# Edge-to-node feature sums by one-hot products: longer alternation of blocks and products, other PSUM banks, GpSimd work in short pieces

## The chip, the cores and the metric

The kernel runs on one core of a Trainium2 chip. The metric is the device time of one execution in microseconds. Of the kernel before, seven runs were timed: the median is 342.38 us, the lowest 340.65 and the highest 344.02.

## What is computed

```python
# num_nodes, num_edges, dim = 4096, 65536, 128; float32 features
output = np.zeros((num_nodes, dim), dtype=np.float32)
for i in range(len(edge_index_src)):
    output[edge_index_dst[i]] += node_features[edge_index_src[i]]
```

Each edge adds the feature row of its source node to the row of its destination node. Both are random numbers below 4096, that is, one of 32 blocks of 128 nodes.

## The kernel before

The kernel has no gather. It sorts the edges so that TensorE can do the sum as a matrix product. **Pass 1** (up to about 70 us) moves each edge to a row that belongs to its destination block, and **pass 2** moves it on by source block. What then remains of an edge is a pair of numbers below 128, source and destination within their blocks. VectorE turns such numbers into one-hot matrices: a comparison of a row 0..127 with each number (`onehot`, L201).

The **main loop** goes over 32 slots (from L585), one for each of the 32 destination blocks. For a slot TensorE does two things.

- `blocks(k)`, k from 0 to 7, is four matmuls 128x128 of one-hots (bf16, L532). They fill one PSUM bank `psa` with four count matrices (how many edges go from source to destination, for four source blocks). ScalarE copies the bank to SBUF as fp32r, `a[:, k, :]` (L534).
- `product(k)` is two matmuls 128x512 in fp32r (L539): the node features (`xr`, in a high and a low part) times `a`. They add up in the bank `pso` over four slots' worth of source blocks: 64 matmuls, then ScalarE copies the bank out (`evacuate`, L298). Later `finish` transposes it with four matmuls into `psx` (L305), ScalarE copies that to `rows` (L307), and SyncE sends it to HBM.

The products lag by one slot: in slot s TensorE works on the blocks of slot s and the products of slot s-1. The order is written by hand: blocks k and k+1 (eight matmuls), products k and k+1 (four matmuls), four times over. `finish` stands behind the first such pair of steps. So TensorE changes between blocks and products four times each way in a slot.

VectorE makes the two one-hot tensors of slot s+1 while slot s runs (`onehots`, two instructions 128x4096, L201). They go to two tiles in turn, so VectorE has to wait until the blocks of slot s-1 have been read.

**Pass 2 runs inside the main loop.** Its 32 positions are cut into `GROUPS` of 4, 4, 4, 4, 8 and 8. `STEPS` says by hand in which slot a group's next step is issued. A step has a VectorE half, which is issued ahead of the slot's blocks, and a TensorE half, which is issued behind the slot's products. For a group of 4 the steps are: one-hots (`buckets4`, L473) and `payloads` (L415), with column sums (L482); scans (L489) with counting matmuls `counts_ranks` (L496, L499; ScalarE copies with L502) and `ranks` (L432); then pairs of `permutations` (VectorE, L201, to `p2a` and `p2c`) and `permuted` (TensorE, L452), followed two slots later by `quad_keys` (VectorE, L465). For a group of 8, `buckets` (32 instructions, L400) and `before_all` (L408) come first, then `running` (eleven VectorE additions, L423) with `masked` (L427) and `payloads`, then `ranks`, then four pairs. Group 0 and the first two steps of group 1 run ahead of the loop.

GpSimd has `masked` and, from group 1 on, `payloads`. One `payloads` instruction multiplies 128x3072 bf16 elements, one `masked` instruction 128x6144. They are one instruction each, or two `payloads` for a group of 8.

PSUM has eight banks, which the pool `ps` gives out by tag, with two buffers unless told otherwise: `psA` (blocks, and the counting banks `psc` of both passes) two, `pso` (products, and `pst` and `psr` of pass 1) two, `misc` (`psm`, `psb`, `psr2`, `pst2`, `psx`, `psf`) two, `psi` one, `ps2` one. A matmul that writes a bank anew waits until its last reader is done.

Of the kernel before, what the change touches and what calls it, by code (L numbers as in the profile page):

```python
# [8 lines left out]
P = 128  # L9
F32 = mybir.dt.float32  # L10
# [7 lines left out]
NB = 32  # L18
# [60 lines left out]
def _fast(ctx, tc, X, src32, dst32, out, ident, fmax, flag_i, T):  # L79
# [129 lines left out]
    def oh1s(q):  # L209

        if q % 2 == 0:
            oh1[q // 2] = sb1.tile([P, 2, NL, NB], BF16, name="oh1", tag=f"o{q // 2}")
        onehot(oh1q(q), kd[:, q], NL, NB)
        pst = ps.tile([P, 512], F32, name="pst", tag="pso")
        for j in range(NJ):
            PE.matmul(out=pst[:, j:j + 1],  # L216
                      lhsT=oh1q(q)[:, 4 * j:4 * j + 4, :].rearrange("p l b -> p (l b)"),
                      rhs=ones[:, :1], start=True, stop=True)
        sums[q] = pst
# [8 lines left out]
    def counts(q):  # L228

        cum = sb1.tile([P, NB, NL], BF16, name="cum", tag=f"c{q % 2}")  # L230
        for j0 in range(0, NJ, 4):
            n = min(4, NJ - j0)
            psc = ps.tile([P, 512], F32, name="psc", tag="psA")
            PE.matmul(out=psc[:, :n * P], lhsT=early[:],  # L234
                      rhs=oh1q(q)[:, 4 * j0:4 * (j0 + n), :].rearrange("p t b -> p (t b)"),
                      start=True, stop=j0 + n == 1)
            for j in range(max(j0, 1), j0 + n):
                PE.matmul(out=psc[:, (j - j0) * P:(j - j0 + 1) * P],  # L238
                          lhsT=sums[q][:, j - 1:j].to_broadcast([P, P]), rhs=identb[:],
                          start=False, stop=j == j0 + n - 1)  # L240
            S.activation(out=cum[:, :, 4 * j0:4 * (j0 + n)], func=RELU, bias=minus[:],  # L241
                         in_=psc[:, :n * P].rearrange("p (t b) -> p b t", b=NB))
            yield
        psr = ps.tile([P, 512], F32, name="psr", tag="pso")
        for b in range(NB):
            PE.matmul(out=psr[:, :NL], lhsT=identb[:], rhs=cum[:, b, :],  # L246
                      start=b == 0, stop=b == NB - 1)
        rank1[q] = sb2.tile([P, 4, NJ, 2], BF16, name="rank1", bufs=3)
        for k in range(2):
            S.copy(out=rank1[q][:, :, :, k], in_=psr[:, :NL].rearrange("p (j l) -> p l j", l=4))  # L250
# [23 lines left out]
    sbk = sb1.tile([P, NCH, NB], BF16, name="sbk")  # L274

    def move1(q, meanwhile):
        psm = ps.tile([P, 512], F32, name="psm", tag="misc")
        for l in range(4):
            t = p1[l // 2]
            n = len([j for j in range(NJ) if j * NCH + q * 4 + l < T])  # L280
            for j0, j1, m0, m1 in WIN:
                j1 = min(j1, n)
                onehot(t[:, l % 2, j0:j1, m0:m1], rank1[q][:, l, j0:j1], j1 - j0, m1 - m0, m0=m0)
            meanwhile(l)
            for j in range(n):
# [14 lines left out]

    def finish():
        for k, res in done:
            psx = ps.tile([P, 512], F32, name="psx", tag="misc")
            for i in range(4):
                PE.transpose(psx[:, i * P:(i + 1) * P], res[:, i * P:(i + 1) * P], ident[:])  # L305
            rows = sb2.tile([P, 4, P], F32, name="rows", bufs=1)
            S.copy(out=rows[:].rearrange("p i f -> p (i f)"), in_=psx[:])  # L307
            nc.sync.dma_start(
                out=out[4 * k * P:4 * (k + 1) * P, :].rearrange("(i p) f -> p i f", p=P),
                in_=rows[:])  # L310
        done.clear()
# [56 lines left out]
    first = [sum(GROUPS[:g]) for g in range(len(GROUPS))]  # L368
    keys2 = {}

    def pass2(g):


# [7 lines left out]
        def flat2(t):  # L381
            return t.rearrange("p c i s k -> p c (i s k)")
# [19 lines left out]
                    in_=sbk[:, :, ds].rearrange("p c (i k) -> p c i k", k=kk))  # L402

        def before_all():
            psb = ps.tile([P, 512], F32, name="psb", tag="misc")
            for h in range(2):
                for c in range(NH):
                    PE.matmul(out=psb[:, h * W:(h + 1) * W], lhsT=before[:],  # L408
                              rhs=flat2(T2["o"])[:, h * NH + c], start=c == 0, stop=c == NH - 1)
            for h in range(2):  # L410
                S.copy(out=flat2(T2["c"])[:, h * NH], in_=psb[:, h * W:(h + 1) * W])

        def payloads():
            for i in range(gk):
                (V if g == 0 else G).tensor_tensor(out=T2["v"][:, :, i], in0=T2["o"][:, :, i], op=OP.mult,  # L415
                                in1=sa[:, :, None, d0 + kk * i:d0 + kk * i + kk].to_broadcast(
                                    [P, NCH, NB, kk]))

        def running():
            cums = flat2(T2["c"]).rearrange("p (h c) w -> p h c w", h=2)  # L420
# [3 lines left out]
                                op=OP.add)  # L424

        def masked():
            G.tensor_tensor(out=flat2(T2["c"]), in0=flat2(T2["c"]), in1=flat2(T2["o"]), op=OP.mult)  # L427

        def ranks():
            psr = ps.tile([P, 512], F32, name="psr2", tag="misc")  # L430
            for s in range(NB):
                PE.matmul(out=psr[:, :NCH * gd], lhsT=identb[:],  # L432
                          rhs=T2["c"][:, :, :, s, :].rearrange("p c i k -> p (c i) k"),
                          start=s == 0, stop=s == NB - 1)
            T2["r"] = sb2.tile([P, gd, NCH, 2], BF16, name="rank2")
            for k in range(2):
                S.copy(out=T2["r"][:, :, :, k],  # L437
                       in_=psr[:, :NCH * gd].rearrange("p (c d) -> p d c", d=gd))
# [5 lines left out]
                    onehot(p2b[d % 4][:, cs, h * 64:h * 64 + 64], T2["r"][:, d, cs], NH, 64)  # L444

        def permuted(i):
            if i % 4 == 0:
                T2["ps2"] = ps.tile([P, 512], F32, name="ps2", tag="ps2", bufs=1)
            ps2 = T2["ps2"]
            for d in range(i, i + 2):  # L450
                for c in range(NCH):
                    PE.matmul(out=ps2[:, d % 4 * NB:(d % 4 + 1) * NB],  # L452
                              lhsT=p2b[d % 4][:, c, :], rhs=T2["v"][:, c, d // kk, :, d % kk],
                              start=c == 0, stop=c == NCH - 1)
            if i % 4 == 2:
                T2["pa"] = sb2.tile([P, NB, 4], BF16, name="pa")
                S.copy(out=T2["pa"][:],
                       in_=ps2[:, :4 * NB].rearrange("p (d s) -> p s d", d=4))
# [18 lines left out]
                in1=sbk[:, :, None, d0:d0 + 4].to_broadcast([P, NCH, NB, 4]))  # L477

        def column_sums():
            T2["p"] = ps.tile([P, 512], F32, name="pst2", tag="misc")  # L480
            for c in range(NCH):
                PE.matmul(out=T2["p"][:, c:c + 1], lhsT=flat2(T2["o"])[:, c], rhs=ones[:, :1],  # L482
                          start=True, stop=True)
# [7 lines left out]

        def counts_ranks():
            for c0 in range(0, NCH, 4):
                psc = ps.tile([P, 512], F32, name="psc2", tag="psA")
# [32 lines left out]
        return oh  # L527

    def blocks(k, oh, a):
        psa = ps.tile([P, 512], F32, name="psa", tag="psA")  # L530
        for i in range(4):
            PE.matmul(out=psa[:, i * P:(i + 1) * P], lhsT=oh[:, 0, 4 * k + i, :],  # L532
                      rhs=oh[:, 1, 4 * k + i, :], start=True, stop=True)
        S.copy(out=a[:, k, :], in_=psa[:])  # L534
# [7 lines left out]
    def flag():  # L542
# [10 lines left out]
        psf = ps.tile([P, 512], F32, name="psf", tag="misc")  # L553
# [6 lines left out]
    def run(fs):  # L560
        for f in fs:
            f()
# [22 lines left out]
    for slot in range(slots):  # L585
# [5 lines left out]
        if slot + 1 < slots:  # L591
            oh = onehots(slot + 1)
        run(st[0] for st in steps)
        a = sb1.tile([P, 8, 4 * P], F32R, name="a", tag=f"A{slot % 2}")
        if slot % 4 == 0:
            pso = ps.tile([P, 512], F32, name="pso", tag="pso")
        for k in range(0, 8, 2):
            blocks(k, cur, a)
            blocks(k + 1, cur, a)
            if prev is not None:  # L600
                product(k, *prev)
                product(k + 1, *prev)
            if k == 0:
                finish()
        if prev is not None and prev[0] % 4 == 3:
            evacuate(prev[0] // 4, prev[2])
        run(st[1] for st in steps if len(st) > 1)
# [98 lines left out]
```

## Time and profile before

| what | value |
| --- | --- |
| the profiled execution's own time | 342.22 us |
| its span, first to last instruction | 340.5 us |
| median of the seven runs | 342.38 us |
| mean granted TensorE clock | 0.969 |
| TensorE matmuls busy | 302.6 us |
| VectorE busy | 280.4 us |
| ScalarE busy | 201.6 us |
| GpSimd busy | 84.0 us |
| `product` matmuls (L539) | 512, 149.3 us busy |
| `blocks` matmuls (L532) | 1024, 81.2 us busy |
| copies of a block bank (L534) | 256, mean 591 ns |
| one-hots of a slot (L201) | 2 of 128x4096, mean 2287 and 2280 ns |

In the profile, PE is TensorE's matmuls, PEld its weight loads, DVE is VectorE, ACT ScalarE, POOL GpSimd. "L539" is a line of the kernel before. In a list of groups or a timeline, a line gives start and duration in us (or the sum of busy time and the mean), engine, line, operation, the tiles (written <- read), the shape, and the number of instructions. In square brackets stands the time for which the engine was idle before, and whose work ended that. Matmuls overlap: the duration of one is longer than the distance to the next. So distances between starts are what counts on TensorE.

### The profile page before, as it was taken

To read this page: it belongs to the slowest core of one execution; us is meant where nothing else is said; L and a number is where in the kernel's file an instruction comes from. 1 tells how busy PE (TensorE), PEld (TensorE's weight loads), DVE (VectorE), ACT (ScalarE), POOL (GpSimd) and SP (SyncE) were. 2 spreads that over 40 slices of the span, in tenths; PEclk is the share of its full clock that TensorE was granted. 3 is DMA by queue.
4 is the path that set the end of the run, shared out by engine and by line. 5 is a ranking of instruction groups with operands and counts; after the bars stand their busy time and mean duration, and the time that the engine had idled before them with its cause. 6 is when DMAs were issued, how large, how long until landed. Compare 5 with 4: busy or idle time off the path is not lost.

```text
span 340.5 us, 8629 instructions
## 1 busy us (share of the span) xinstructions
PE 302.6 (89%) x3783; PEld 239.9 (70%) x3784; DVE 280.4 (82%) x365; ACT 201.6 (59%) x389; POOL 84.0 (25%) x47
## 2 busy tenths in 40 slices
PE   0579898558879999999999999999999999999993
PEld 0368787456668678677788787778878778877772
DVE  4999999981899839868999898999999779858710
ACT  2776545014455766755755766575576676677761
POOL 6627000206006060000799000059900000000000
PEclk9999979975799999999999999999999999999999
DMA  8500000000000000100010000001000100100101
GB/s 241 128 2 5 2 3 2 2 2 0 3 2 2 2 2 2 31 2 3 0 33 2 0 6 30 0 3 33 2 1 2 33 0 2 33 2 0 33 2 33
DMA packets 8711, 5.81 MB, mean 17 GB/s; under 512 B 224, under 2 KB 8416, under 8 KB 8672
## 3 DMA queue, kind: packets, MB, share of 16 engines
q1 hardware_dynamic: 8528, 4.72, 4.8%
q8 instruction: 30, 0.49, 0.6%
q10 hardware_dynamic: 144, 0.52, 0.5%
q14 instruction: 9, 0.07, 0.1%
HBM read 3.15 MB, written 2.10 MB: 15 GB/s over the span
## 4 chain that ended last, share of the span: by engine, by line
PE 69%; DVE 19%; ACT 5%; issue 5%; DMA 1%; DVEq 0%; ACTq 0%
PE pso L539 33%; PE psa L532 15%; DVE oh L201 8%; PE ps L452 7%; PE psr L432 3%; PE psm L286 3%; DVE p L201 2%; DVE v L262 2%; ACT cum L502 2%; DMA raw<-in_edge_index_dst_dram 1%; DVE cum L423 1%; ACT cum L241 1%; PE psc L496 1%; PE psr L246 1%; PE psc L499 1%
## 5 line engine op out<-in xcount | busy, mean ns | idle before, releaser
L534 ACT CAST a<-psa 128x512 fp32r<-128x512 f32 x256 | 137.7, 591 | 46.0 <-PE psa L532 45.0
L539 PE MATMUL pso<-a,xr 128*128 128x512 f32 x512 | 149.3, 414 | 0.0
L201 DVE TENSOR_TENSOR oh<-psi,slo 128x4096 bf16<-128x4096 uint16 x32 | 73.2, 2287 | 27.9 <-PE psa L532 27.8
L539 PEld LDWEIGHTS pso<-a,xr 128*128 128x128 f32 x512 | 87.0, 189 | 11.3
L532 PE MATMUL psa<-oh 128*128 128x128 bf16 x1024 | 81.2, 220 | 1.4 <-ACT a L534 0.9
L532 PEld LDWEIGHTS <-oh 128*128 128x128 bf16 x1024 | 59.3, 98 | 29.9 <-issue 28.4
L201 DVE TENSOR_TENSOR oh<-psi,dlo 128x4096 bf16<-128x4096 uint16 x32 | 73.0, 2280 | 0.0
L415 POOL TENSOR_TENSOR v<-oh,sa 128x3072 bf16<-128x3072 bf16 x7 | 37.6, 5391 | 41.8 <-DVE oh L473 33.6
L427 POOL TENSOR_TENSOR cum<-cum,oh 128x6144 bf16<-128x6144 bf16 x2 | 23.9, 11930 | 75.7 <-ACT a L534 75.7
L201 DVE TENSOR_TENSOR p<-psi,rank 128x448 bf16<-128x448 uint16 (+3 forms) x72 | 29.2, 471 | 0.0
L241 ACT ACTIVATE cum<-psc,minus 128x512 bf16<-128x512 f32 (+1 forms) x36 | 21.8, 650 | 10.4 <-PE psc L238 9.9
L286 PE MATMUL psm<-v,p 128*128 128x64 bf16 x512 | 22.7, 202 | 5.6 <-DVE p L201 5.0
L286 PEld LDWEIGHTS <-p 128*128 128x128 bf16 x512 | 19.6, 103 | 7.5 <-DVE p L201 7.2
L201 DVE TENSOR_TENSOR p2a<-psi,rank 128x768 bf16<-128x768 uint16 x32 | 15.5, 548 | 7.2 <-ACT rank L437 7.2
L201 DVE TENSOR_TENSOR p2c<-psi,rank 128x768 bf16<-128x768 uint16 x32 | 15.5, 547 | 0.0
L238 PEld LDWEIGHTS <-sums 128*128 128x128 bf16 x126 | 10.9, 105 | 6.5 <-issue 3.2
L234 PE MATMUL psc<-oh,early 128*128 128x512 bf16 (+1 forms) x36 | 14.4, 399 | 1.0 <-ACT cum L241 1.0
L432 PEld LDWEIGHTS <-identb 128*128 128x128 bf16 x192 | 12.3, 103 | 4.2 <-issue 4.2
L190 POOL TENSOR_TENSOR xr<-xf,xr 128x512 fp32r<-128x512 f32 x8 | 11.7, 1488 | 13.4 <-ACT xr L186 13.4
L216 PE MATMUL pst<-ones,oh 128*128 128x1 bf16 x132 | 4.3, 164 | 12.0 <-DVE oh L201 12.0
L452 PEld LDWEIGHTS <-p2a 128*128 128x128 bf16 x384 | 12.8, 100 | 2.9 <-DVE p2a L201 1.8
L452 PEld LDWEIGHTS <-p2c 128*128 128x128 bf16 x384 | 12.9, 102 | 1.9 <-issue 1.6
(82 smaller groups left out, 278.0 us busy)
## 6 DMA issues: line engine op xcount, KB each, us to landing
xf<-in_node_features_dram SPq DMA_DIRECT2D x4, 512.0 KB, 7.4
out_dram<-rows SPq DMA_DIRECT2D x8, 256.0 KB, 2.3
raw<-in_edge_index_src_dram ACTq DMA_DIRECT2D x1, 512.0 KB, 4.8
raw<-in_edge_index_dst_dram SPq DMA_DIRECT2D x1, 512.0 KB, 5.1
```

What stands on the lines that cost most here:

```text
L190: G.tensor_tensor(out=xr[i // 2][:, bs, 1, :], op=OP.subtract, in0=xf[i][:, h * BX // 2:(h + 1) * BX // 2], in1=xr[i // 2][:, bs, 0, :])
L201: V.tensor_tensor(out=dst.rearrange("p i (m k) -> p i m k", k=2), in0=io.rearrange("p i (m k) -> p i m k", k=2), in1=keys2[:, :, None, :]. ...
L234: PE.matmul(out=psc[:, :n * P], lhsT=early[:], rhs=oh1q(q)[:, 4 * j0:4 * (j0 + n), :].rearrange("p t b -> p (t b)"), start=True, stop=j0 + ...
L241: S.activation(out=cum[:, :, 4 * j0:4 * (j0 + n)], func=RELU, bias=minus[:], in_=psc[:, :n * P].rearrange("p (t b) -> p b t", b=NB))
L286: PE.matmul(out=psm[:, l * 64:(l + 1) * 64], lhsT=t[:, l % 2, j, :], rhs=v1[q][:, 4 * j + l].rearrange("p k b -> p (k b)"), start=j == 0, ...
L415: (V if g == 0 else G).tensor_tensor(out=T2["v"][:, :, i], in0=T2["o"][:, :, i], op=OP.mult, in1=sa[:, :, None, d0 + kk * i:d0 + kk * i + ...
L427: G.tensor_tensor(out=flat2(T2["c"]), in0=flat2(T2["c"]), in1=flat2(T2["o"]), op=OP.mult)
L432: PE.matmul(out=psr[:, :NCH * gd], lhsT=identb[:], rhs=T2["c"][:, :, :, s, :].rearrange("p c i k -> p (c i) k"), start=s == 0, stop=s == N ...
L452: PE.matmul(out=ps2[:, d % 4 * NB:(d % 4 + 1) * NB], lhsT=p2b[d % 4][:, c, :], rhs=T2["v"][:, c, d // kk, :, d % kk], start=c == 0, stop=c ...
L532: PE.matmul(out=psa[:, i * P:(i + 1) * P], lhsT=oh[:, 0, 4 * k + i, :], rhs=oh[:, 1, 4 * k + i, :], start=True, stop=True)
L534: S.copy(out=a[:, k, :], in_=psa[:])
L539: PE.matmul(out=pso[:], lhsT=xr[s // 16][:, s % 16, v, :], rhs=a[:, k, :], start=s == 0 and v == 0, stop=s == NB - 1 and v == 1)
```

## The change

The diff has three parts.

1. **Order in the slot.** Four `blocks` (sixteen matmuls), then four `products` (eight matmuls), twice over. `finish` moves from behind the first two products to between the second four blocks and the second four products. The matmuls and their number stay.
2. **Banks.** `psA` gets four banks, `pso` and `misc` one each. In pass 1, `pst` goes to `ps2` and `pso` in turn, and `psr` to `psA`.
3. **GpSimd in pieces.** `payloads` is cut into pieces of four chunks (six of 128x512 for each 128x3072), `masked` into pieces of two chunks (twelve of 128x512). They go to a list `small`; the program issues up to seven of them in each slot, behind the VectorE halves, and what `ranks` or `permuted` needs, ahead of those. Group 0's payload stays one VectorE instruction.

```diff
@@ oh1s, counts, move1, finish, before_all, ranks, column_sums, flag: banks
-        pst = ps.tile([P, 512], F32, name="pst", tag="pso")
+        pst = ps.tile([P, 512], F32, name="pst", tag=("ps2", "pso")[q % 2], bufs=1)
-            psc = ps.tile([P, 512], F32, name="psc", tag="psA")
+            psc = ps.tile([P, 512], F32, name="psc", tag="psA", bufs=4)
-        psr = ps.tile([P, 512], F32, name="psr", tag="pso")
+        psr = ps.tile([P, 512], F32, name="psr", tag="psA", bufs=4)
-        psm = ps.tile([P, 512], F32, name="psm", tag="misc")
+        psm = ps.tile([P, 512], F32, name="psm", tag="misc", bufs=1)
...
+    small = []
+
+    def little(n=0, until=None):
+        while small and (n > 0 or any(k == until for k, _ in small)):
+            small.pop(0)[1]()
+            n -= 1
...
+        def payload(e, i, cs):
+            ds = slice(d0 + kk * i, d0 + kk * i + kk)
+            e.tensor_tensor(out=T2["v"][:, cs, i], in0=T2["o"][:, cs, i], op=OP.mult,
+                            in1=sa[:, cs, None, ds].to_broadcast([P, cs.stop - cs.start, NB, kk]))
+
         def payloads():
+            if g == 0:
+                payload(V, 0, slice(0, NCH))
+                return
             for i in range(gk):
-                (V if g == 0 else G).tensor_tensor(out=T2["v"][:, :, i], in0=T2["o"][:, :, i], op=OP.mult,
-                                in1=sa[:, :, None, d0 + kk * i:d0 + kk * i + kk].to_broadcast(
-                                    [P, NCH, NB, kk]))
+                for c in range(0, NCH, 4):
+                    small.append(((g, 1), lambda i=i, c=c: payload(G, i, slice(c, c + 4))))
...
         def masked():
-            G.tensor_tensor(out=flat2(T2["c"]), in0=flat2(T2["c"]), in1=flat2(T2["o"]), op=OP.mult)
+            for c in range(0, NCH, 2):
+                small.append(((g, 0), lambda c=c: G.tensor_tensor(
+                    out=flat2(T2["c"])[:, c:c + 2], in0=flat2(T2["c"])[:, c:c + 2],
+                    in1=flat2(T2["o"])[:, c:c + 2], op=OP.mult)))
         def ranks():
+            little(until=(g, 0))
...
         def permuted(i):
+            little(until=(g, 1))
...
     def blocks(k, oh, a):
-        psa = ps.tile([P, 512], F32, name="psa", tag="psA")
+        psa = ps.tile([P, 512], F32, name="psa", tag="psA", bufs=4)
...
         run(st[0] for st in steps)
+        little(7)
         a = sb1.tile([P, 8, 4 * P], F32R, name="a", tag=f"A{slot % 2}")
         if slot % 4 == 0:
-            pso = ps.tile([P, 512], F32, name="pso", tag="pso")
-        for k in range(0, 8, 2):
-            blocks(k, cur, a)
-            blocks(k + 1, cur, a)
+            pso = ps.tile([P, 512], F32, name="pso", tag="pso", bufs=1)
+        for k0 in (0, 4):
+            for k in range(k0, k0 + 4):
+                blocks(k, cur, a)
+            if k0 == 4:
+                finish()
             if prev is not None:
-                product(k, *prev)
-                product(k + 1, *prev)
-            if k == 0:
-                finish()
+                for k in range(k0, k0 + 4):
+                    product(k, *prev)
```

More of the change, by code (lines that the diff above doesn't have):

```diff
@@ L302, in finish @@
         for k, res in done:
-            psx = ps.tile([P, 512], F32, name="psx", tag="misc")
+            psx = ps.tile([P, 512], F32, name="psx", tag="misc", bufs=1)
             for i in range(4):
@@ L404, in before_all @@
         def before_all():
-            psb = ps.tile([P, 512], F32, name="psb", tag="misc")
+            psb = ps.tile([P, 512], F32, name="psb", tag="misc", bufs=1)
             for h in range(2):
@@ L426, in masked @@
         def masked():
-            G.tensor_tensor(out=flat2(T2["c"]), in0=flat2(T2["c"]), in1=flat2(T2["o"]), op=OP.mult)
+            for c in range(0, NCH, 2):
+                small.append(((g, 0), lambda c=c: G.tensor_tensor(
+                    out=flat2(T2["c"])[:, c:c + 2], in0=flat2(T2["c"])[:, c:c + 2],
+                    in1=flat2(T2["o"])[:, c:c + 2], op=OP.mult)))
         def ranks():
-            psr = ps.tile([P, 512], F32, name="psr2", tag="misc")
+            little(until=(g, 0))
+            psr = ps.tile([P, 512], F32, name="psr2", tag="misc", bufs=1)
             for s in range(NB):
@@ L479, in column_sums @@
         def column_sums():
-            T2["p"] = ps.tile([P, 512], F32, name="pst2", tag="misc")
+            T2["p"] = ps.tile([P, 512], F32, name="pst2", tag="misc", bufs=1)
             for c in range(NCH):
@@ L493, in counts_ranks @@
             for c0 in range(0, NCH, 4):
-                psc = ps.tile([P, 512], F32, name="psc2", tag="psA")
+                psc = ps.tile([P, 512], F32, name="psc2", tag="psA", bufs=4)
                 cs = [c for c in range(c0, c0 + 4) if c % NH]
@@ L552, in flag @@
         V.tensor_reduce(out=fall[:], in_=fmax[:, :ng + 1], op=OP.add, axis=AX.X)
-        psf = ps.tile([P, 512], F32, name="psf", tag="misc")
+        psf = ps.tile([P, 512], F32, name="psf", tag="misc", bufs=1)
         PE.matmul(out=psf[:1, :1], lhsT=fall[:], rhs=one[:], start=True, stop=True)
```

## The prediction

> **What bounds the kernel now.** I read the page first: shares, slices, chain.
>
> ```profile
> PE 302.6 (89%) x3783; PEld 239.9 (70%) x3784; DVE 280.4 (82%) x365; ACT 201.6 (59%) x389; POOL 84.0 (25%) x47
> ...
> PE   0579898558879999999999999999999999999993
> ...
> DVE  4999999981899839868999898999999779858710
> ...
> PE 69%; DVE 19%; ACT 5%; issue 5%; DMA 1%; DVEq 0%; ACTq 0%
> ```
>
> PE is full from about 120 us on, the chain of waits is mostly PE. But two engines are nearly full, so I asked for busy time in stretches of 10 us (PE, PEld, DVE, ACT, POOL, clock):
>
> ```profile
> 60.00:70.00 10.00, 6.57 (x126) 5.47 (x126) 10.00 (x21) 0.43 (x2) 2.78 (x4) 0.85 0.01 2
> ...
> 270.00:280.00 10.00, 10.00 (x85) 7.59 (x84) 6.54 (x7) 7.46 (x15) 0.00 (x0) 1.00 0.00 0
> ```
>
> Pass 1 is VectorE's, the main loop TensorE's. A busy PE may still have gaps, so I went through the starts in a slot without pass-2 work:
>
> ```profile
> 272.90 0.62 PE L532 MATMUL psa<-oh 128*128 128x128 bf16 x8
> 273.33 1.18 PE L539 MATMUL pso<-a,xr 128*128 128x512 f32 x4
> 274.35 0.62 PE L532 MATMUL psa<-oh 128*128 128x128 bf16 x8
> 274.78 1.17 PE L539 MATMUL pso<-a,xr 128*128 128x512 f32 x4
> ```
>
> A round takes 1.447 us, four rounds make a slot of 5.79. Single matmuls in the trace start as follows. Block to block: 0.066 once, then 6 x 0.056. Last block to first product: 0.028. First to second product: **0.315** (124 of them, 0.315 to 0.316). Next two: 0.231 each. Last product to next block: 0.239. Sum 1.447. The first product is late by 0.085 against the others. Its weights take 189 ns (the groups' mean for L539; 98 for L532) and have only a block of 56 ns to hide behind; the second product waits in turn.
>
> **Part 1, the order.** A round of eight blocks and four products becomes half of one of sixteen and eight: 0.066 + 14 x 0.056 + 0.028 + 0.315 + 6 x 0.231 + 0.239 = 2.818 against 2.894. So a change that goes saves 0.075. Two go per slot with products, slots 1 to 31: 62 x 0.075 = **-4.65**. Bounds: if long runs go at the rate of the sixteen products that end the kernel (single starts 0.227 apart, inside this line of the chain), 0.10 each, -6.2;
>
> ```profile
> 329.96 4.63 PE pso L539 x20
> ```
>
> if the late weights come back in some other form, 0. I take 0.075, from 124 records of the same pair.
> The Trainium skill weighs this lower: "TensorE: Matmul & The Clock Gate", section "LDWEIGHTS (loading the stationary operand)", gives columns / 1.2 ns, 107 ns for 128, whatever is loaded. By it only 107 - 56 = 51 ns (an estimate) would be exposed and part 1 be worth 3.2 us; the trace has 189 ns for these weights, so I keep to it.
>
> **Part 2, the banks.** Four for blocks. With two, a round gives ScalarE 1.447 us for two copies that need about 1.07 in sequence; anything else on ScalarE makes TensorE wait. That is seen behind each `finish` inside the loop; first PE, then ACT:
>
> ```profile
> 289.71 1.17 PE L539 MATMUL pso<-a,xr 128*128 128x512 f32 x4
> 290.73 0.76 PE L532 MATMUL psa<-oh 128*128 128x128 bf16 x8
> ```
> ```profile
> 289.49 0.59 ACT L307 COPY rows<-psx 128x512 f32<-128x512 f32 x1 [0.51 <-PE psx L305]
> 289.97 2.26 ACT L534 CAST a<-psa 128x512 fp32r<-128x512 f32 x4
> ```
>
> Eight blocks take 0.76 instead of 0.62: 0.145 lost, seven times, 1.0 us. The same gap stands at 159.4 (0.26, ScalarE copies L411), 189.0 (0.13) and 249.1 (0.21): 0.6 us. With four banks a bank has 2.8 us for its copy: **-1.6**.
> Where ScalarE itself is the limit nothing is won. In slots 2 and 5 `counts_ranks` has TensorE waiting 1.43 us, but the six copies L502 run without a gap (4.01 us). Slot 0's copies bind too, and behind it TensorE waits for VectorE's L473 anyway.
> In pass 1, one wait of VectorE hangs on a bank; PE, then DVE:
>
> ```profile
> 22.82 0.38 PE L234 MATMUL psc<-oh,early 128*128 128x512 bf16 x1 [0.34 <-ACT cum L241]
> ```
> ```profile
> 23.82 0.20 DVE L225 TENSOR_TENSOR_SCAN sums<-ones,pst 128x22 bf16<-128x22 bf16 x1 [0.54 <-PE psc L238]
> ```
>
> VectorE is full from there to 70.4, so this counts: 0.34 to 0.54, I take **-0.4**.
> The single banks add waits. (a) `pso`: the first product of a new sum waits for the copy L298. At the end of the kernel that copy is done 1.06 us after the last product's start (334.18 to 335.25). Between that start and the next first product lie 0.24 + sixteen blocks, 1.12 us, and in six of seven cases `permuted` (1.5 us) besides: 0, at worst some 0.5 each if ScalarE is behind. Behind the waiting product stand the slot's other products; the blocks are ahead of it. (b) `misc`: `psm` of the next quarter waits for L290 and L291; `counts` or VectorE's one-hots lie between, at most 0.1 at 33.8. Group 1's column sums (83.26) wait for the copies L437, done at 83.91; they then end near 84.6, where the next matmul waits for VectorE: **+0.05**. In slot 5 `psx` needs the scan of group 3 (137.5 now, some 1.5 earlier then) and comes at about 138.5: 0.
> `finish` itself moves. Its four transposes then stand between a block and a product with long weights; a second late load may cost up to 0.15, seven times. Bounds 0 and +1.0; **+0.5**.
>
> **Where VectorE is close behind.** TensorE waits for it in slot 16:
>
> ```profile
> 229.35 1.94 PE L452 MATMUL ps<-v,p2a 128*128 128x32 bf16 x48 [0.27 <-DVE p2a L201]
> ```
>
> VectorE has no idle time from 206.14 to there; it started when slot 13's blocks were read. After the change eight products instead of four follow a slot's last block (1.97 us instead of 1.05), so VectorE starts 0.92 earlier against TensorE, while its 23.2 us stay. Slots 14 to 16 can win 0.92 and no more: 0.45 of it is in part 1, so **-0.48**. In slots 7 and 8 the same sum leaves 0.7 us to spare: `running` waits for the copies L411, which I put 5.05 us after slot 6's blocks; with it (4.94), a slot's one-hots (4.4) and the first L201 to `p2a` (0.6) VectorE is ready after 15.0, TensorE comes after 4.4 + 2 x 5.64 = 15.7.
>
> **Part 3, GpSimd.** It works beside the loop; what it costs is nothing while it is in time. Now:
>
> ```profile
> 163.98 11.94 POOL L427 TENSOR_TENSOR cum<-cum,oh 128x6144 bf16<-128x6144 bf16 x1 [37.41 <-ACT a L534]
> 175.87 10.76 POOL L415 TENSOR_TENSOR v<-oh,sa 128x3072 bf16<-128x3072 bf16 x2
> ```
> ```profile
> 181.32 5.46 DVE L465 TENSOR_SCALAR dlo<-pa 128x256 uint16<-128x256 uint16 x1
> ```
>
> `dlo` takes 0.29 otherwise. Here it ends with GpSimd's instruction (186.63): it was shut out. In pieces it waits for one piece, about 1 us; 4 to 5 us of VectorE come free here and at 242. But VectorE has 1.2 and 0.5 us idle right behind, so now this costs TensorE nothing: **0**; it keeps VectorE in time for slot 20, which otherwise would be about even.
> A piece has 512 columns: 1/6 of 5.38 is 0.90, 1/12 of 11.93 is 0.99, plus a start. Memsets on GpSimd bound that: 0.15 for 56 columns. The dearest row of this size is L190 (fp32), 1.49. I take 1.05, nearest to the row of the same operation. A group of 8 needs 24 pieces. Between the first and `permuted`'s need lie 199.1 - 164.0 and 259.4 - 225.0, less the 1.2 and 1.1 by which TensorE gets there earlier (five slots at 0.15 and the stalls): 33.9 and 33.3 us. So a piece may cost 1.4 before anyone waits; at 1.49 the loss is 4.3 in all.
> [...]
>
> **The sum.** -4.65 - 1.6 - 0.4 + 0.05 + 0.5 - 0.48 = -6.6. The profiled execution took 342.22, its span 340.5; the rest stays. So 335.6. The median of the runs, 342.38, is 0.16 above it, which I neglect.
>
> **Rivals.**
> 1. *VectorE takes the place of TensorE* in slots 7 to 10 and 14 to 20. For: it is 97 to 100% busy from 160 to 260, and the waits at 229. Against: 1 us earlier starts, up to 10 us less shutting out. Price: eleven slots x 0.15, and the stalls there that part 2 would remove (0.26 + 0.13 + 0.21 + two of 0.145): 2.5, so 338.1.
> 2. *The change doesn't do what it says*: the late load isn't tied to the change of kind but comes back inside runs of eight. For: weights of 189 ns are close to the 231 between products. Against: the last sixteen products show no such gap. Price: part 1 is 0 and single banks eat some of the rest: 341.
> 3. *Slower: GpSimd comes late.* At p us a piece both groups lose 48p - 67.2 together. It eats the 6.6 from p = 1.54, and at 1.6 gives 342.2 - 6.6 + 9.6 = 345.2. For: the start of an instruction is not known, and VectorE shuts GpSimd out too (one L262 beside it, at 30.08, took 2.69, elsewhere 1.61: they want something in common). Against: it has to exceed the dearest row of this size, 1.49.
>
> **Chances.** Forecast, 333.5 to 337.3: 0.62. Rival 1 (337.3 to 340.5): 0.25. Rival 2: 0.07. Rival 3: 0.06. A measurement here tells about 0.5% (1.7 us) from no change. Faster 0.87, same 0.07, slower 0.06. The range must leave out 0.2 at most. Low end: part 1 at 0.10 each (-6.2), 0 for `finish`, the scan at 0.54, the rest as above, -8.2, and about 1 for the spread of the runs: 333.0. High end, within rival 1: 339.0.
>
> **What would show it.** Step 1: rounds of about 2.82 us and 62 late products instead of 124. Step 2: no wait of L532 for L534 in slots 1 to 31, and first products of slots 5, 9 ... 29 on time. `finish`: distance from a second block group to its products. VectorE: the wait in slot 16 stays. GpSimd: pieces of 0.9 to 1.2, `dlo` at most about 1. The prediction is wrong if runs of sixteen blocks or eight products are slower per matmul than runs of eight and four, if `pso` waits, or if `permuted` waits for GpSimd.

## The result and the profile after

The changed kernel takes a median of **343.49 us** (26 runs, 341.95 to 344.92), the kernel before 342.26 (63 runs). The ratio is **1.0031, 95% interval 1.0014 to 1.0048**: 0.3% slower, where 335.6 was predicted. The profiled execution took 342.98 us, its span is 341.3.

In the changed kernel the lines are numbered anew: `blocks` are L552, their copies L554, products L559, `permuted` L472, `running` L438, `masked` L443, `payloads` L423, `quad_keys` L485. The page of the changed kernel:

```profile
PE 296.2 (87%) x3778; PEld 247.4 (72%) x3784; DVE 284.1 (83%) x365; ACT 194.6 (57%) x389; POOL 94.5 (28%) x104
...
PEclk9999999878787999999979999997999999999998
...
PE 59%; DVE 25%; issue 8%; ACT 4%; DMA 1%; DVEq 0%; ACTq 0%
...
L438 DVE TENSOR_TENSOR cum<-cum,oh 128x512 bf16<-128x512 bf16 x22 | 16.1, 731 | 1.5 <-ACT cum L419 0.8
```

TensorE's share of the chain fell from 69 to 59%, VectorE's rose from 19 to 25%. The last line is `running`: 22 additions, 731 ns each; in the kernel before they took 425 (9.4 us in all). The row of granted clocks has new dips, in the middle of the main loop too.

The plain slots did become shorter. PE in one of them:

```profile
274.10 1.07 PE L552 MATMUL psa<-oh 128*128 128x128 bf16 x16
274.98 2.09 PE L559 MATMUL pso<-a,xr 128*128 128x512 f32 x8
276.91 1.07 PE L552 MATMUL psa<-oh 128*128 128x128 bf16 x16
```

Half a slot takes 2.81 us between starts, a slot 5.61 to 5.63, against 5.79. To see where that went, I took the distance between the first blocks of successive slots in both traces (us):

| slots | before | after | difference |
| --- | --- | --- | --- |
| up to slot 0 | 95.20 | 93.17 | -2.03 |
| 0 | 7.37 | 7.69 | +0.32 |
| 1 | 7.31 | 9.74 | **+2.43** |
| 8 | 7.28 | 10.48 | **+3.20** |
| 9 | 7.86 | 8.45 | +0.59 |
| 16 | 7.99 | 10.87 | **+2.88** |
| 17 | 7.87 | 8.33 | +0.46 |
| 22 (plain) | 5.78 | 5.61 | -0.17 |
| 25 (with `finish`) | 7.88 | 7.55 | -0.33 |

Most other slots win 0.15 to 0.43 (slots 2 and 5 win 0.61 and 0.77). Three stretches lose, and they give all of it back.

Not all of the 2.03 us ahead of slot 0 belongs to the change. The 32 matmuls of group 0's `ranks` fell into a stretch at half clock in the kernel before, and into one at full clock in the changed kernel; before, then after:

```profile
80.74 2.72 PE L432 MATMUL psr<-vc,identb 128*128 128x96 bf16 x32 [0.78 <-ACT vc L502]
```
```profile
80.16 1.53 PE L451 MATMUL psr<-vc,identb 128*128 128x96 bf16 x32 [0.78 <-ACT vc L522]
```

Those 1.2 us differ from one execution to the next: three of the experiments below (e1, e10, e13) are the same program up to slot 0 and start it at 94.43, 93.06 and 92.82.

**Slots 8 and 16.** VectorE, then GpSimd, then PE, in the changed kernel:

```profile
157.62 8.40 DVE L438 TENSOR_TENSOR cum<-cum,oh 128x512 bf16<-128x512 bf16 x11 [0.84 <-ACT cum L419]
165.93 2.28 DVE L201 TENSOR_TENSOR oh<-psi,slo 128x4096 bf16<-128x4096 uint16 x1
```
```profile
158.65 1.34 POOL L443 TENSOR_TENSOR cum<-cum,oh 128x512 bf16<-128x512 bf16 x1 [31.73 <-DVE cum L438]
160.34 1.41 POOL L443 TENSOR_TENSOR cum<-cum,oh 128x512 bf16<-128x512 bf16 x1 [0.36 <-DVE cum L438]
```
```profile
170.94 1.94 PE L472 MATMUL ps<-v,p2a 128*128 128x32 bf16 x48 [2.92 <-DVE p2a L201]
```

The eleven additions took 5.02 before:

```profile
158.78 5.02 DVE L423 TENSOR_TENSOR cum<-cum,oh 128x512 bf16<-128x512 bf16 x11
```

Now the first mask piece begins one microsecond into them, as soon as the first columns have their sums; each further piece waits for the next columns, so pieces and additions interleave. Single additions show the price of one piece:

```profile
158.99 1.27 DVE L438 TENSOR_TENSOR cum<-cum,oh 128x512 bf16<-128x512 bf16 x1
```
```profile
160.30 0.42 DVE L438 TENSOR_TENSOR cum<-cum,oh 128x512 bf16<-128x512 bf16 x1
```

An addition that begins while a piece runs ends 0.28 us behind it and takes 1.27. The next begins just ahead of GpSimd's next piece (160.30 and 160.34) and takes 0.42; there it is the piece that takes longer, 1.41 instead of the 1.15 of pieces that meet no addition. Each engine holds the other up, whichever comes second. Four additions of 1.27 for 0.42 are 3.4 us, which is the whole stretch from 5.0 to 8.4. VectorE is that much late with `p2a`, and TensorE waits 2.92 us (3.30 in slot 16). The one-hots (L201, 2.28) next to pieces are as long as ever.

**Slot 1.** Busy time in stretches of 3.4 us (PE, PEld, DVE, ACT, POOL, clock), changed kernel:

```profile
92.80:96.20 3.40, 2.95 (x45) 2.29 (x41) 3.40 (x2) 2.84 (x8) 0.00 (x0) 1.00 0.00 0
96.20:99.60 3.40, 1.93 (x48) 1.68 (x48) 3.40 (x6) 1.47 (x3) 0.00 (x0) 1.00 0.00 0
99.60:103.00 3.40, 2.81 (x41) 2.77 (x42) 3.40 (x3) 1.52 (x4) 2.72 (x3) 0.51 0.03 7
103.00:106.40 3.40, 3.40 (x12) 2.34 (x11) 3.39 (x5) 0.53 (x2) 3.36 (x4) 0.50 0.00 0
```

Behind a stretch in which PE was busy for 1.93 of 3.40 us, the clock is halved for two stretches. With four banks slot 0's blocks are done early, and TensorE then waits for VectorE in two pieces (0.99 and 1.13 us); between them stand only 48 matmuls of `permuted`, each with 32 columns. Before, with two banks, small waits for copies spread the blocks out, twelve of them fell into the stretch of `permuted`, and no stretch there had less than 2.27. Busy time alone isn't what decides, though. In the same trace, two stretches and what followed each:

```profile
82.57:85.98 3.41, 3.32 (x93) 3.12 (x90) 3.41 (x10) 0.00 (x0) 0.22 (x1) 1.00 0.02 5
85.98:89.40 3.42, 3.20 (x38) 2.42 (x36) 2.40 (x5) 1.72 (x4) 0.00 (x0) 0.50 0.01 2
144.01:147.42 3.41, 1.95 (x51) 1.95 (x51) 3.39 (x29) 1.79 (x5) 0.00 (x0) 1.00 0.00 0
147.42:150.83 3.41, 3.41 (x58) 3.15 (x56) 0.66 (x3) 2.28 (x6) 0.00 (x0) 1.00 0.02 5
```

Behind 3.32 us of matmuls with 32 columns or one the clock fell; behind 1.95 us, most of it matmuls with 96 columns, it stayed whole. The last section counts the columns. The waits of slots 8 and 16 have the same sequel: 3.4 us at half clock in slots 9 and 17.

### The profile page after: what moved, and what is told of

It is laid out like the page before. It is cut to its first block, busy times and chain, and to the rows that moved or that the text cites. A ratio compares the mean times of both kernels' runs of the same rounds, so it can differ in the third digit from the quotient of the medians.

```text
span 341.3 us, 8685 instructions
## 1 busy us (share of the span) xinstructions
PE 296.2 (87%) x3778; PEld 247.4 (72%) x3784; DVE 284.1 (83%) x365; ACT 194.6 (57%) x389; POOL 94.5 (28%) x104
## 3 DMA queue, kind: packets, MB, share of 16 engines
HBM read 3.15 MB, written 2.10 MB: 15 GB/s over the span
## 4 chain that ended last, share of the span: by engine, by line
PE 59%; DVE 25%; issue 8%; ACT 4%; DMA 1%; DVEq 0%; ACTq 0%
PE pso L559 30%; PE psa L552 15%; DVE oh L201 8%; PE ps L472 7%; DVE p L201 5%; DVE cum L438 5%; DVE v L262 4%; PE psr L451 3%; ACT cum L522 2%; DMA raw<-in_edge_index_dst_dram 1%; PE psx L305 1%; DVE oh L493 1%; DVE p2a L201 1%; PE psc L519 1%; PE pst L502 1%
## 5 line engine op out<-in xcount | busy, mean ns | idle before, releaser
L554 ACT CAST a<-psa 128x512 fp32r<-128x512 f32 x256 | 131.6, 603 | 52.4 <-PE psa L552 52.3
L559 PE MATMUL pso<-a,xr 128*128 128x512 f32 x512 | 135.3, 407 | 0.0
L559 PEld LDWEIGHTS pso<-a,xr 128*128 128x128 f32 x512 | 93.0, 191 | 17.2
L201 DVE TENSOR_TENSOR oh<-psi,slo 128x4096 bf16<-128x4096 uint16 x32 | 73.2, 2286 | 24.4 <-PE psa L552 24.0
L201 DVE TENSOR_TENSOR oh<-psi,dlo 128x4096 bf16<-128x4096 uint16 x32 | 73.0, 2281 | 0.0
L552 PE MATMUL psa<-oh 128*128 128x128 bf16 x1024 | 71.2, 224 | 0.4
L552 PEld LDWEIGHTS <-oh 128*128 128x128 bf16 x1024 | 60.4, 100 | 12.2 <-issue 11.9
L423 POOL TENSOR_TENSOR v<-oh,sa 128x512 bf16<-128x512 bf16 x42 | 42.5, 1045 | 40.3 <-DVE oh L493 32.0
L443 POOL TENSOR_TENSOR cum<-cum,oh 128x512 bf16<-128x512 bf16 x24 | 29.5, 1250 | 68.1 <-DVE cum L438 34.6
L201 DVE TENSOR_TENSOR p<-psi,rank 128x448 bf16<-128x448 uint16 (+3 forms) x72 | 29.2, 473 | 0.0
L241 ACT ACTIVATE cum<-psc,minus 128x512 bf16<-128x512 f32 (+1 forms) x36 | 21.4, 654 | 10.4 <-PE psc L238 10.3
L201 DVE TENSOR_TENSOR p2a<-psi,rank 128x768 bf16<-128x768 uint16 x32 | 15.5, 549 | 5.7 <-ACT rank L456 5.7
L472 PEld LDWEIGHTS <-p2a 128*128 128x128 bf16 x384 | 13.1, 102 | 9.7 <-DVE p2a L201 8.2
L472 PE MATMUL ps<-v,p2a 128*128 128x32 bf16 x336 | 12.5, 195 | 7.2 <-DVE p2a L201 7.2
L438 DVE TENSOR_TENSOR cum<-cum,oh 128x512 bf16<-128x512 bf16 x22 | 16.1, 731 | 1.5 <-ACT cum L419 0.8
L451 PEld LDWEIGHTS <-identb 128*128 128x128 bf16 x192 | 11.1, 96 | 6.1 <-issue 6.1
L201 DVE TENSOR_TENSOR p2c<-psi,rank 128x768 bf16<-128x768 uint16 x32 | 15.5, 548 | 0.0
```

Source lines behind the costliest of these rows:

```text
L201: V.tensor_tensor(out=dst.rearrange("p i (m k) -> p i m k", k=2), in0=io.rearrange("p i (m k) -> p i m k", k=2), in1=keys2[:, :, None, :]. ...
L423: e.tensor_tensor(out=T2["v"][:, cs, i], in0=T2["o"][:, cs, i], op=OP.mult, in1=sa[:, cs, None, ds].to_broadcast([P, cs.stop - cs.start, N ...
L438: V.tensor_tensor(out=cums[:, :, c], in0=cums[:, :, c - 1], in1=ohs2[:, :, c - 1], op=OP.add)
L443: small.append(((g, 0), lambda c=c: G.tensor_tensor(out=flat2(T2["c"])[:, c:c + 2], in0=flat2(T2["c"])[:, c:c + 2], in1=flat2(T2["o"])[:, ...
L451: PE.matmul(out=psr[:, :NCH * gd], lhsT=identb[:], rhs=T2["c"][:, :, :, s, :].rearrange("p c i k -> p (c i) k"), start=s == 0, stop=s == N ...
L472: PE.matmul(out=ps2[:, d % 4 * NB:(d % 4 + 1) * NB], lhsT=p2b[d % 4][:, c, :], rhs=T2["v"][:, c, d // kk, :, d % kk], start=c == 0, stop=c ...
```

## The experiments

Theory A: mask pieces begin while `running` is at work and shut it out. Theory B: pieces are dear as such. Theory C: the half clock in slot 1 cancels the gain. Times are medians; each ratio is against the kernel before on the same chip (medians 342.1 to 342.4; e12 and e13 are single runs without a ratio).

### e1_masks_last_first

```diff
-            for c in range(0, NCH, 2):
+            for c in reversed(range(0, NCH, 2)):
```

> The changed kernel with one word more: the twelve mask pieces of a group are issued from the last columns to the first, so that the first of them needs the last of the eleven running sums and none can begin before VectorE is through with them. Theory A (overlap): mask pieces that run beside the running sums stretch these from 5.0 to 8.4 us in both groups of 8, and TensorE then waits 2.9 and 3.3 us and goes at half clock for a while (0.9 and 0.8). Then the sums take 5.0 us again, the two waits shrink to under 0.5 and the time falls by 6 to 8, to about 335 to 337. Theory B (pieces as such): a mask piece costs 1.25 us instead of 1.0, so GpSimd is late whatever the order: then it stays at 343. Theory C (clock): what cancels the gain is the half clock in slot 1 (2.4 us); then this changes under 1 us.

Measured: 341.98, ratio 0.9979 (0.995 to 1.0009). `running` takes 5.02 and 5.00 again, and slots 8 and 9 take 7.12 and 7.55: theory A's link is right, and B is out as the cause of what slots 8 and 9 lost.

```profile
158.86 5.02 DVE L438 TENSOR_TENSOR cum<-cum,oh 128x512 bf16<-128x512 bf16 x11 [0.84 <-ACT cum L419]
```

But the time fell by 1.5, not by 6 to 8: a new wait took the place of the old one. GpSimd, VectorE, then PE:

```profile
164.05 13.50 POOL L443 TENSOR_TENSOR cum<-cum,oh 128x512 bf16<-128x512 bf16 x12 [35.91 <-DVE cum L438]
177.49 12.13 POOL L423 TENSOR_TENSOR v<-oh,sa 128x512 bf16<-128x512 bf16 x12
```

```profile
180.70 9.07 DVE L485 TENSOR_SCALAR slo<-pa 128x256 uint16<-128x256 uint16 x1
189.69 0.28 DVE L485 TENSOR_SCALAR dlo<-pa 128x256 uint16<-128x256 uint16 x1
```
```profile
194.59 1.07 PE L552 MATMUL psa<-oh 128*128 128x128 bf16 x16 [2.39 <-DVE oh L201]
```

`slo` of `quad_keys`, an instruction of 0.28 us, begins at 180.70 while GpSimd has nine payload pieces to go, the one at work included, and ends at 189.77, 0.15 behind the last of them (189.62). VectorE doesn't get in between the pieces of this row. The next one-hots are late, and TensorE waits 2.39 us for them (2.27 in slot 19), and 0.84 in slot 16. In the changed kernel itself the same happens (4.25 and 4.24 us, to the last piece), but there VectorE has the time.

### e2_mask_pieces_alone

```diff
 (kernel before)
-            G.tensor_tensor(out=flat2(T2["c"]), in0=flat2(T2["c"]), in1=flat2(T2["o"]), op=OP.mult)
+            for c in range(0, NCH, 2):
+                G.tensor_tensor(out=flat2(T2["c"])[:, c:c + 2], in0=flat2(T2["c"])[:, c:c + 2],
+                                in1=flat2(T2["o"])[:, c:c + 2], op=OP.mult)
```

> The kernel before, and of the change only the mask in twelve pieces, issued at once where the one mask stood; order, banks and payloads as before. Theory A (overlap): the running sums go from 5.0 to 8.4 us twice, TensorE waits about 3 us in slots 8 and 16 and falls to half clock after it: 342.3 plus 6 to 8, about 349. Theory B (a piece costs 1.25 us): 24 pieces end about 4 us later than the two masks did, still ahead of what needs them: 342.3. Theory C: no effect on slot 1, 342.3.

Measured: 351.11, ratio 1.0236 (1.0174 to 1.0298), +8.8 us. `running` and TensorE's wait (here `running` is L423, `permuted` L454):

```profile
158.81 8.39 DVE L423 TENSOR_TENSOR cum<-cum,oh 128x512 bf16<-128x512 bf16 x11
```
```profile
172.12 1.94 PE L454 MATMUL ps<-v,p2a 128*128 128x32 bf16 x48 [2.33 <-DVE p2a L201]
```

This one cut alone costs what the changed kernel fell short by. Slot 16 waits 3.64, and slots 9 and 17 lose 0.9 and 1.1 to half clock. Theory A holds; B and C, which expected no change here, fall as the main cause.

### e3_order_banks_alone

The changed kernel, with `payloads` and `masked` as they were before.

> The changed kernel with GpSimd's masks and payloads whole as in the kernel before: the order of blocks and products and the PSUM banks alone. The prediction's parts 1 and 2 (fewer late products, a bank in time) give 342.3 minus 6.6, 335.6, and if TensorE falls to half clock in slot 1 as in the changed kernel, 338. Theory A expects that, with running sums of 5.0 us. If order and banks are worth nothing after all, 342 to 343.

Measured: **334.98**, ratio 0.9758 (0.9698 to 0.9818). Order and banks alone give 7.4 us, 0.8 more than the 6.6 predicted (the interval, 6.2 to 10.3 us, holds both), although slot 1 takes 9.95 us, at half clock. `running` takes 5.03. The wait in slot 16 stays, as predicted (0.76).

### e4_filler_slot0

```diff
+    def filler(n):
+        psz = ps.tile([P, 512], F32, name="psz", tag="psA", bufs=4)
+        for i in range(n):
+            PE.matmul(out=psz[:, i % 4 * P:(i % 4 + 1) * P], lhsT=identb[:], rhs=identb[:],
+                      start=True, stop=True)
...
+        (slot 0: filler(16) ahead of each TensorE half of a step)
```

> The changed kernel with 32 more matmuls 128x128 in slot 0, whose result nobody reads: sixteen ahead of each of the two places where TensorE waits for VectorE there (0.99 and 1.13 us). Theory C (clock): the half clock from 99.6 to 106.4 follows these waits; without them slot 1 takes 7.1 to 7.3 us instead of 9.7 and the time falls by 2 to 2.5, to 341. If the half clock has another cause, slot 1 stays at 9.7 and the time at 343 to 344 (the matmuls need 1.8 us, at half clock 3.4, in waits of 2.1). Theory A says nothing on slot 1; it expects slots 8 and 16 as long as before.

Measured: 340.65, ratio 0.9942 (0.9907 to 0.9977), against 1.0031 without. PE around slot 1 (the unread matmuls are L581):

```profile
97.50 1.05 PE L581 MATMUL psz<-identb 128*128 128x128 bf16 x16
98.39 1.93 PE L472 MATMUL ps<-v,p2a 128*128 128x32 bf16 x48
100.16 1.06 PE L581 MATMUL psz<-identb 128*128 128x128 bf16 x16
101.44 0.75 PE L502 MATMUL pst<-ones,oh 128*128 128x1 bf16 x24 [0.23 <-DVE oh L493]
102.06 1.05 PE L552 MATMUL psa<-oh 128*128 128x128 bf16 x16
102.92 2.06 PE L559 MATMUL pso<-a,xr 128*128 128x512 f32 x8
104.83 1.07 PE L552 MATMUL psa<-oh 128*128 128x128 bf16 x16
```

Slot 1 takes 7.12 instead of 9.74, and the granted clock stays whole from 90.6 to 169.1, where the wait of slot 8 halves it again. Matmuls that compute nothing win about 2.8 us, by keeping TensorE at work. So theory C is right about slot 1, and its price is 2.6; slots 8 and 16 are as long as before (10.47, 10.85).

### e5_whole_and_filler

Order and banks alone (e3) with the filler of e4.

> Order and banks alone with GpSimd's work whole, and the 32 matmuls nobody reads in slot 0. If the two causes (GpSimd's pieces, the half clock in slot 1) add up, then slot 1 takes 7.1 instead of 9.95 and the time is 335.0 minus 2.5 to 2.8, about 332.4. If the filler's gain of the last run belonged to something else in the pieces' kernel, it stays at 335.

Measured: 332.24, ratio 0.9706 (0.9672 to 0.974); slot 1 takes 7.15. The two causes add up.

### e6_payload_pieces

The changed kernel, with `masked` whole as before.

> The changed kernel with the masks whole; only the payloads are in pieces. Theory D: pieces that follow each other at once shut VectorE's quad_keys out until the last of them is done, as the run with the masks from the last columns suggests (9.07 us, ending with the last piece). Then the first quad_keys behind each group of 8 again takes 5 to 8 us, not 1, and ends with GpSimd's last piece; TensorE may wait up to 1 us for it: 335.0 to 336.5. The prediction's view (VectorE gets in after one piece): quad_keys take at most 1.1 us each, time 334 to 335.

Measured: 334.58, ratio 0.9762 (0.9731 to 0.9794). Here VectorE does get in: `slo` takes 0.45 and `dlo` 1.13, about one piece, as the prediction had it, and slot 16 has no wait (7.50). My theory D, as I had put it, falls: that pieces follow each other at once isn't enough to shut VectorE out. GpSimd, then VectorE:

```profile
174.86 12.22 POOL L423 TENSOR_TENSOR v<-oh,sa 128x512 bf16<-128x512 bf16 x12
```
```profile
179.64 0.45 DVE L482 TENSOR_SCALAR slo<-pa 128x256 uint16<-128x256 uint16 x1
180.01 1.13 DVE L482 TENSOR_SCALAR dlo<-pa 128x256 uint16<-128x256 uint16 x1
```

### e7_banks_alone

e3 with the order of the kernel before (pairs of blocks and products, `finish` behind the first pair).

> The banks of the change alone: order of blocks and products and place of the transposes as before, GpSimd's work whole. Part 2 of the prediction gives -1.6 in the loop; with slot 0's blocks done earlier TensorE waits at a stretch there, and if that is what halves the clock (theory C), slot 1 takes 9.5 to 10 instead of 7.3: 342.3 - 1.6 + 2.5, about 343. Without the half clock 340 to 341. The rest down to 335.0, 5 to 8, is then the order's.

Measured: 341.95, ratio 1.0001 (0.9978 to 1.0023). Slot 1 takes 9.58, so it is the banks that bring the half clock, by letting slot 0's blocks finish early. With the old order the single banks do make TensorE wait (PE, slots 5 and 29):

```profile
137.75 0.66 PE L305 MATMUL psx<-ident,res 128*128 128x128 f32 x4 [0.83 <-DVE sums L499]
...
312.54 1.20 PE L549 MATMUL pso<-a,xr 128*128 128x512 f32 x4 [0.21 <-ACT res L298]
```

Neither is there in e3. So the order, with `finish` further back, is worth the 7 us between e7 and e3: 0.16 in most slots, and these waits (slot 5 takes 1.23 less in e3, slot 29 0.61).

### e8_pieces_apart

```diff
 (e1)
             small.pop(0)[1]()
+            G.iota(apart[:], pattern=[[1, 32]], base=0, channel_multiplier=0)
```

> The kernel with the mask pieces from the last columns to the first, and behind each piece one small iota on GpSimd, which reads nothing from SBUF. Theory D: quad_keys get in only where GpSimd has a gap between its pieces; the iota makes one, so slo takes at most about 2 us instead of 9.07 and the waits of 2.39 and 2.28 us in slots 11 and 19 go: 342.0 - 4.5, 337 to 338, unless the 24 iotas of 0.1 to 0.2 us make GpSimd late. If GpSimd keeps VectorE out for as long as anything is queued on it, slo takes 9 us or more again and the time stays at 342 or rises.

Measured: 334.22, ratio 0.9759 (0.9726 to 0.9793), 7.8 us less than e1. `slo` takes 0.50, `dlo` 1.22; slots 11, 16 and 19 have no waits. In the profiles slots 11, 14, 16 and 19 account for 6.3 us; another 1.7 lies ahead of slot 0, where the clock of e1's execution was halved for longer (17.1 us against 6.8 from 73 to 91 us), and isn't the iota's. Some 0.12 us of GpSimd behind each piece is enough to let VectorE in. The kernel's pieces can be harmless, then, if they begin behind `running` and don't stand in one row.

### e9, e10, e12, e13: the moment or the row

In e6 `slo` came 0.75 us behind a piece's start, in e1 0.18, so the moment could have decided. One or two more comparisons on VectorE ahead of the two `quad_keys` shift it.

```diff
+            if (g, i) in ((3, 0), (4, 4)):
+                for _ in range(2):              # e9 (on e6), e10 (on e1); range(1): e12 (e6), e13 (e1)
+                    onehot(shift[:], T2["r"][:, 0, :7], 7, 64)
```

> The kernel with whole masks and payloads in pieces, in which quad_keys got in after 0.45 us, with two more VectorE comparisons 128x448 (0.3 us each, result unused) ahead of the two quad_keys that meet GpSimd's pieces. They shift slo from 0.75 us behind a piece's start to about 0.35. If the moment within a piece decides whether VectorE gets in, slo is now shut out to the last piece (6 us or more). If the stream ahead decides (after a whole mask VectorE gets in, after a dozen mask pieces it doesn't), slo again takes at most about 1.2 us. The time moves little either way, 334 to 336.

> The kernel with the mask pieces from the last columns to the first, in which slo took 9.07 us, with the same two VectorE comparisons ahead of these two quad_keys. They shift slo from 0.18 us behind a piece's start to about 0.8. If the moment within a piece decides, VectorE gets in at the next piece, slo takes about 0.5 and the waits of 2.39 and 2.28 us in slots 11 and 19 go: 337 to 338. If the stream ahead decides, slo is shut out to the last piece again (about 8.5 us) and the time is 342 or a little more.

> Whole masks, payloads in pieces, and one VectorE comparison (0.36 us) ahead of the two quad_keys instead of two or none. So far slo got in when it came 0.45 to 0.75 us behind a piece's start, and was shut out at 0.17 to 0.32 and 0.91 to 0.99; but all cases of the first kind also had no dozen mask pieces ahead. Here it should come at about 0.1. If the moment decides, it is shut out to the last piece (6 us or more); if the stream ahead decides, it gets in within about 1.2 us.

> Mask pieces from the last columns to the first and one VectorE comparison ahead of the two quad_keys. slo should come at about 0.55 us behind a piece's start. If the moment decides, it gets in within a piece (0.5 to 0.6 us) and the time is 337 to 338; if the stream ahead decides, it is shut out to the last piece, 8 to 9 us, and the time is about 341.

| kernel | row ahead on GpSimd | `slo` behind a piece's start, us | `slo` takes, us | time, us |
| --- | --- | --- | --- | --- |
| e9 | one whole mask, payload pieces | 0.46, 0.45 | 0.77, 0.75 | 334.07 |
| e12 | the same | 0.02, 0.04 | 1.20, 1.18 | 336.2 (one run) |
| e10 | twelve mask pieces, payload pieces | 0.91, 0.91 | 8.35, 8.33 | 340.62 |
| e13 | the same | 0.48, 0.48 | 8.79, 8.78 | 340.94 (one run) |

e9 and e13 come at the same moment, and one gets in, the other doesn't. The moment is out: what stands ahead on GpSimd decides, in these kernels. VectorE in e13 and in e12:

```profile
179.30 8.79 DVE L489 TENSOR_SCALAR slo<-pa 128x256 uint16<-128x256 uint16 x1
```
```profile
180.99 1.20 DVE L486 TENSOR_SCALAR slo<-pa 128x256 uint16<-128x256 uint16 x1
```

The ratios of e9 and e10 are 0.9762 (0.9714 to 0.981) and 0.9961 (0.9926 to 0.9996). What a long row of pieces changes inside GpSimd stays open; whether it needs mask pieces, or only more than a handful of any, wasn't tried.

### e11_apart_and_filler

e8 with the filler of e4.

> The version that should be best: mask pieces from the last columns to the first, a small iota behind each piece, and the 32 matmuls nobody reads in slot 0. The two gains add up if the causes are apart: 334.2 minus 2.3 to 2.7 (slot 1 at 7.1 instead of 9.4), 331.7, against 332.2 with GpSimd's work whole, whose slot 16 has a wait of 0.72 that this version doesn't have.

Measured: **331.46**, ratio 0.9685 (0.9656 to 0.9714), 3.15% faster than the kernel before and ahead of both kernels of the comparison. Against e5 (332.24) the intervals overlap, so that pieces done well are worth something isn't settled; slot 16 is 0.8 us shorter here.

## Why the prediction was wrong

**What bounds the kernel**: right. TensorE bounds the loop; VectorE is close behind. That VectorE was close was the reason that 3.4 us on it came through almost whole.

**Part 1, the order**: right, and too low. Half a slot takes 2.81 (2.82 predicted); a slot wins 0.17, not 0.15. The first product of a group is still late by 0.08 (0.315 against 0.231), once in eight products instead of once in four. The Trainium skill's 107 ns for 128 columns of weights ("TensorE: Matmul & The Clock Gate", "LDWEIGHTS (loading the stationary operand)") would have given less; the group of L559 again shows 191 ns, and the measured gain sides with it.

**Part 2, the banks**: right about the loop: no wait of `blocks` for a copy is left behind slot 0. The single banks cost nothing with the new order. Too small or wrong in size: the moved transposes cost 0, not +0.5 (slot 29 takes 6.02, 0.40 above a plain slot); slots 2 and 5 won 0.4 more than other slots of their kind, where I had 0; the scan in pass 1 won 0.23, not 0.4. The -0.48 for slots 14 to 16 doesn't show: they take 22.16 us in e3 against 22.66, which is the order's 0.17 a slot and no more. Taken together, the sum for parts 1 and 2, -6.6, came near e3's -7.4, but in part by luck: in the profiles e3 loses 2.8 in slots 0 and 1, where the sum had -0.15, and wins 1.8 ahead of slot 0 (up to 1.2 of it by where the half clock fell) and 7.5 from slot 2 on, where it had 0.35 and 6.1. The low end of the range was added up wrongly: its terms make -8.8, not -8.2. It changes nothing here.

**Missing from the sum: the clock.** "the rest stays" was wrong for slot 1: 2.6 us lost at half clock (e4; the slot takes 9.4 to 10.0 us in all ten of these kernels that have four banks and no filler). The prediction counted slot 0's four banks as worth nothing, since TensorE waits for VectorE there anyway. It didn't ask what the longer wait does to the clock.

**Part 3, GpSimd: the step that failed.** "It works beside the loop; what it costs is nothing while it is in time." GpSimd was in time: where they meet nothing, mask pieces take 1.16 and payload pieces 1.04 us (I had 1.05, with 1.4 as the most that makes nobody wait), and no wait of TensorE for GpSimd stands in the trace. The price fell on VectorE. I took `running`'s 4.94 us over unchanged, though the cut lets the first masks begin before `running` ends; the whole mask could not. Four meetings in each group make it 8.4 (e2, e1). Slots 8, 9, 16 and 17 then lose 7.6 against e3, and this is the 7.3 us between the spans of e3 (334.0) and the changed kernel (341.3). Rival 3 had the sign and not the mechanism: GpSimd late. The row for it was in its own text: L262, two operands in SBUF, 2.69 beside GpSimd and 1.61 alone. Rival 1 had VectorE in TensorE's place, but by the load it already had, and for 2.5 us.

"In pieces it waits for one piece" was wrong as well for this kernel: `slo` waited for four, to the end of the row. It cost nothing here, as VectorE had time to spare, but 4.7 us in e1.

The Trainium skill states the rule that would have warned: "SBUF — State Buffer", section "SBUF: two separate sides", has one pair of SBUF ports shared by VectorE and GpSimd, which a VectorE instruction with two SBUF operands and a GpSimd instruction that reads SBUF can only hold in turn, for an instruction's whole length. The additions agree (0.42 alone, 1.27 when one begins beside a piece of 1.34), and so do the one-hots with one operand in PSUM (2.28 either way). It says nothing on a whole row of instructions holding out, as in e1.

## What to carry to other kernels

Cutting an instruction changes when its first part can begin: look at what it will then run beside, and whether the two shut each other out, before counting it as hidden. TensorE made faster may get a slower clock, when what is left in a stretch is a wait and some narrow matmuls; here a wait spread out among blocks was cheaper. And measure the parts of a change apart in the first runs: here two parts of opposite sign, 7.4 and 8.5 us, looked like a change that does nothing.

## What the runs showed of the hardware

- The granted clock changes in stretches of 3.4 us (6.8 at half clock in slot 1, 3.4 behind slots 8 and 16). It fell to half behind stretches in which PE was busy for 1.93 of 3.40 us (slot 0) or idle for 2.9 (slot 8), and stayed whole behind stretches with 2.27 to 2.73 (kernel before, 90.9 to 104.5). The Trainium skill ("TensorE: Matmul & The Clock Gate", "What's actually happening") speaks of an idle window of about 3.4 us; here one that was 57% busy was enough.
- What tells these stretches apart is the columns of the matmuls that begin in them, added up (an instruction 128x32 has 32). In the fifteen profiles, from where the record of the clock begins (16 to 22 us), 1197 stretches at full clock can be counted, and 80 were followed by half clock. All 80 had 2880 columns or fewer (slot 0's in the changed kernel 1536); all the others had 3072 or more, but for one of 2560 near the end of the kernel before (four products and four transposes). Busy time doesn't sort them: the clock fell behind 3.32 us (82.6 in the changed kernel) and stayed whole behind 1.50 (191.0 in e13). The filler of e4 adds 29 matmuls of 128 columns to slot 0's stretch. This is a count made afterwards; no run changed the columns alone.
- VectorE's additions with both operands in SBUF, and `slo` and `dlo` of `quad_keys`, are held up while a GpSimd multiplication runs (0.42 to 1.27 us; 0.28 to as much as 9.07). Comparisons with one operand in PSUM aren't, nor is the reduction behind `quad_keys`, though its one operand is in SBUF (0.24 us beside a piece in e6 and 0.24 alone in the kernel before).
- After a row of twelve mask pieces VectorE got in only behind the last of twelve payload pieces (e1, e10, e13, and the changed kernel); after one whole mask, or with an iota of 0.15 us between pieces, it got in after at most one (e6, e8, e9, e12).
